# A block for overfull experts moves in front of expert 29 of a 32-expert layer

## The chip, the cores and the metric

One core of one Trainium2 chip runs one program. The metric is the device time of one execution in microseconds (us). An execution is profiled once more; its time and its span (first to last instruction) are given below.

## The reference

One layer of a flow-matching backbone on 256 latent tokens and 256 context tokens, width 1024. The first sub-layer (three token mixers and their merge) is untouched by this change. The second is a mixture of experts on the 256 latent tokens: a router takes the top 4 of 32 experts for each token, and every expert is a clamped SwiGLU with weights of its own.

```python
gate, up = jnp.split(h @ wgu + bgu, 2, axis=-1)      # 1024 -> 2 x 1024
gate = jnp.minimum(gate, SWIGLU_LIMIT)
up = jnp.clip(up, -SWIGLU_LIMIT, SWIGLU_LIMIT)
glu = gate * jax.nn.sigmoid(SWIGLU_ALPHA * gate)
y = ((up + 1) * glu) @ wd + bd                       # 1024 -> 1024
acc = acc + cw[:, None] * y                          # cw is 0 for a token outside the expert
```

All weights are f32, 12 MB for an expert, so the layer reads about 400 MB of expert weights.

## The kernel before, in words

Tokens are packed: an expert works on up to 64 slots (SLOTS). A token's place in an expert is counted by matmuls beforehand (posq); the number of tokens of each expert stands in cnt[0:32], and the largest of them in cnt[32]. A loop written out over the 32 experts, e = 0 to 31 (so "expert 29" is the 30th), does for each:

- gate_up (L1397): 16 steps (8 blocks of 128 rows, 2 column halves) into one PSUM bank, for the first half of gate and up, and 16 for the second; the bias is a matmul that opens the bank (biases, L1391).
- act (L1402 to L1406): the SwiGLU on VectorE (DVE) and ScalarE (ACT); turn (L1411, L1412): two transposes on TensorE (PE) and a copy on ACT.
- down (L1419): 2 times 16 steps into a bank, then spread (L1422 to L1424: DVE, ACT, DVE), which scales the result and splits it into two parts, and scatter (L1431), 8 matmuls that add it to four accumulator banks acc. The scatter of expert e-1 stands behind the first gate_up of expert e (L1496, L1497).
- gather (L1372): packs the tokens of the next pair of experts, inside the down step.
- select (L1364) marks the slots of tokens 65 to 128 of the expert; a run-time branch over PE, DVE and ACT (L1508 and L1524) computes them only where the expert has over 64 tokens.

Weights: a queue written out in order is loaded by SyncE (SP), one DMA of 2 MB for each of an expert's six pieces: gu e,0 to gu e,3 and dn e,0 and dn e,1 (smaller pieces for the last expert). There are nine slots of 2 MB. done(key) frees a slot at the place in the program where its last reader stands, and pump() issues the next DMA of the queue there and then (L166), so SP's instructions stand in that order. A load waits for the readers of its slot and, since DMAs take eight completion counters in turn, for the landing of the DMA eight before it.

Behind the loop stands the block for experts with over 128 tokens (L1565): a branch on most (the register that holds cnt[32], loaded at L1492) on PE, DVE, ACT and SP. Inside it, for each of the 32 experts, is a second branch, 12 DMAs of 1 MB into the free slots (room), and the computation of tokens 129 to 192 and 193 to 256. With these inputs no expert has over 128 tokens, so the block is jumped over. An engine that jumps executes, behind the branch, event-semaphore instructions that wait for a counter to have its value from before the block and then raise it by what the block would have added. Then come the final layer norm on acc (stats3 L1584, norm2 L1591 and L1592, a half on ACT and GpSimd, L1600 and L1602) and four DMAs of the output.

Of the kernel before, what the change touches and what calls it, by code (L numbers as in the profile page):

```python
# [17 lines left out]
ALU = mybir.AluOpType  # L18
AX = mybir.AxisListType
ET = mybir.EngineType  # L20
# [4 lines left out]
NE = 32  # L25
SLOTS = 64
# [91 lines left out]
def kernel(ctx, tc, x, cx, cols, rows, csts, wsm, wgt, bada, brt, sgub, bdn, bgu,  # L118
                           lnr, wad0, wada, win, wbr, wout, wgu, wdn, out):
    nc = tc.nc  # L120
    mm = nc.tensor.matmul
    V, S, G, T = nc.vector, nc.scalar, nc.gpsimd, nc.tensor
# [24 lines left out]
    loaded = {}  # L147
# [31 lines left out]
    def halves(*key):  # L179

        w = weight(key)
        return [w[:, 0:2048], w[:, 2048:4096]]
# [47 lines left out]
    with ExitStack() as p1:  # L230
# [159 lines left out]
        g2q = cst.tile([P, 512], F32, name="g2q")  # L390
# [937 lines left out]
    def sps2():  # L1328
        sbank.append(sbank.pop(0))
        return sbank[-1]  # L1330
# [26 lines left out]
    ysum = Buf(A2, 512)  # L1357
# [5 lines left out]
    def select(sl, n, c, e):  # L1363
        V.tensor_tensor(out=sl, in0=iota[:, None, None, SLOTS * c:SLOTS * c + SLOTS].to_broadcast([P, 2, n, SLOTS]),  # L1364
                        in1=posq[:, :, e:e + n].unsqueeze(3).to_broadcast([P, 2, n, SLOTS]), op=ALU.is_equal)
# [21 lines left out]
    def bias_of(e):  # L1387
        V.tensor_copy(out=bse[e % 2][:].rearrange("p (q n) -> p q n", q=2), in_=bsel[:, e, :].unsqueeze(2).to_broadcast([P, 2, SLOTS]))
# [11 lines left out]
    def act(b, hf, pg):  # L1400
        gc = b["gc"][hf]
        V.tensor_scalar_min(gc[:], pg[:, 0:256], LIMIT)  # L1402
        S.activation(out=sg[:], in_=gc[:], func=AF.Sigmoid, scale=SW_ALPHA)  # L1403
        V.tensor_scalar(out=up[:], in0=pg[:, 256:512], scalar1=LIMIT, scalar2=-LIMIT, op0=ALU.min, op1=ALU.max)  # L1404
        V.tensor_tensor(out=gc[:], in0=gc[:], in1=sg[:], op=ALU.mult)
        V.scalar_tensor_tensor(out=gc[:], in0=up[:], scalar=1.0, in1=gc[:], op0=ALU.add, op1=ALU.mult)  # L1406
# [14 lines left out]
    def spread(b, py):  # L1421
        V.scalar_tensor_tensor(out=ysum[:], in0=py[:], scalar=b["cwv"][:, 0:1], in1=g2q[:], op0=ALU.mult, op1=ALU.mult)  # L1422
        S.copy(out=yhx[:], in_=ysum[:])  # L1423
        V.tensor_tensor(out=ylx[:], in0=ysum[:], in1=yhx[:].bitcast(F32), op=ALU.subtract)  # L1424

    def scatter(b, last=False):
        for t in range(2):
            for hf in range(2):
                sl = slice(64 * hf, 64 * hf + 64)
                for y_ in (yhx, ylx):  # L1430
                    mm(acc[t][hf][:], b["sT"][sl, P * t:P * t + P], y_[sl, :], start=False, stop=last and y_ is ylx,  # L1431
                       skip_group_check=True)
# [12 lines left out]
    def scatter_whole(b, y, last):  # L1445
        for t in range(2):
            for hf in range(2):
                sl = slice(64 * hf, 64 * hf + 64)
                mm(acc[t][hf][:], b["sT"][sl, P * t:P * t + P].bitcast(F32), y[sl, :], start=False, stop=last, skip_group_check=True)

    def rest(e, g, wu, wd, end=False):
        turn(over, 0)
        biases(e, 1, g)
        gate_up(over["hT"][:, :, 0, :], g, range(8), wu)
        act(over, 1, g)
        py = sps2()
        down(over, py, range(4), wd)
        turn(over, 1)
        down(over, py, range(4, 8), wd)
        if end:  # L1460
            V.scalar_tensor_tensor(out=ysum[:], in0=py[:], scalar=over["cwv"][:, 0:1], in1=g2q[:], op0=ALU.mult, op1=ALU.mult)
            scatter_whole(over, ysum, False)
        else:
            spread(over, py)
            scatter(over)


    engs = [ET.PE, ET.DVE, ET.Activation]
# [15 lines left out]
    for e in range(NE):  # L1484
        p = pair[e // 2 % 2]
        q_ = pair[(e // 2 + 1) % 2]
        hT = p["hT"][:, :, e % 2, :]
        w = halves("gu", e, 0) + halves("gu", e, 1)
        select(over["sl"][:], 1, 1, e)
        _, (tv,) = nc.values_load_multi_w_load_instructions(cnt[0:1, e:e + 1], engines=engs, min_val=0, max_val=256)  # L1490
        if e == NE - 1:
            _, (most,) = nc.values_load_multi_w_load_instructions(cnt[0:1, NE:NE + 1], engines=[*engs, ET.SP], min_val=0, max_val=256)  # L1492
        g0, g1 = gbank if e % 2 == 0 else gbank[::-1]
        gate_up(hT, g0, range(8), w)
        act(cur, 0, g0)
        if e:  # L1496
            scatter(cur)  # L1497
        if e == NE // 2:
            for hf in range(2):
                sl = slice(64 * hf, 64 * hf + NE)  # L1500
                V.tensor_tensor(out=bdnt[sl], in0=bdnt[sl], in1=g2q[sl], op=ALU.mult)
        if e == NE - 4:
            for hf in range(2):
                sl = slice(64 * hf, 64 * hf + NE)
                for t in range(2):
                    mm(acc[t][hf][:], cwT[sl, P * t:P * t + P], bdnt[sl], start=False, stop=False, skip_group_check=True)
        over["hT"] = q_["hT"][:, 4:8].rearrange("p k (i j) n -> p (k i) j n", j=1)
        with tc.If(tv > SLOTS):  # L1508
            rest_gate(e, w)
        for i in range(2):  # L1510
            done(("gu", e, i))
        wu = halves("gu", e, 2)
        wu += halves("gu", e, 3) if e < NE - 1 else [weight(("gu1", e, i)) for i in range(2)]
        biases(e, 1, g1)
        gate_up(hT, g1, range(4), wu)
        spots(cur, p["sl"][:, :, e % 2, :], e)
        turn(cur, 0)
        gate_up(hT, g1, range(4, 8), wu)
        act(cur, 1, g1)
        if e < NE - 1:  # L1520
            wd = halves("dn", e, 0) + halves("dn", e, 1)
        else:
            wd = [weight(("dn1", e, i)) for i in range(4)]
        with tc.If(tv > SLOTS):  # L1524
            rest(e, g1, wu, wd)
        for key in [("gu", e, 2), ("gu", e, 3)] if e < NE - 1 else [("gu", e, 2), ("gu1", e, 0), ("gu1", e, 1)]:
            done(key)
        if e + 1 < NE:
            bias_of(e + 1)
        if e % 2 == 0 and e + 2 < NE:  # L1530
            select(q_["sl"][:], 2, 0, e + 2)
        down(cur, g0, range(4), wd)
        for key in [("dn", e, 0)] if e < NE - 1 else [("dn1", e, 0), ("dn1", e, 1)]:
            done(key)
        turn(cur, 1)
        if e + 2 - e % 2 < NE:
            gather(q_, e % 2, 2)
        if e + 1 < NE:
            biases(e + 1, 0, g1)
        down(cur, g0, range(4, 8), wd)  # L1540
        for key in [("dn", e, 1)] if e < NE - 1 else [("dn1", e, 2), ("dn1", e, 3)]:
            done(key)
        if e < NE - 1:
            spread(cur, g0)
        else:
            ylast, lnb = Buf(A, 512), Buf(A, 2, D)
            for i in range(2):
                S.dma_start(out=lnb[:, i, :], in_=lnr[2 + i:3 + i, :].to_broadcast([P, D]))
            V.scalar_tensor_tensor(out=ylast[:], in0=g0[:], scalar=cur["cwv"][:, 0:1], in1=g2q[:], op0=ALU.mult, op1=ALU.mult)
            scatter_whole(cur, ylast, True)  # L1550
        if e == 0:
            for hf in range(2):
                S.dma_start(out=bdnt[64 * hf:64 * hf + NE], in_=bdn[:, 512 * hf:512 * hf + 512])
        if e == NE - 6:
            ps = sps2()
            for hf in range(2):
                for t in range(2):
                    mm(ps[64 * hf:64 * hf + NE, P * t:P * t + P], cw[:, t], ident[:], start=True, stop=True)
            for hf in range(2):
                V.tensor_copy(out=cwT[64 * hf:64 * hf + NE], in_=ps[64 * hf:64 * hf + NE, 0:256])  # L1560

    engs = [*engs, ET.SP]
    room = [sp.slot() for sp in spaces for _ in range(sp.wlimit)]
    room = [r for r in room if r is not None]
    with tc.If(most > 2 * SLOTS):  # L1565
        for e in range(NE):
            _, (tv,) = nc.values_load_multi_w_load_instructions(cnt[0:1, e:e + 1], engines=engs, min_val=0, max_val=256)
            with tc.If(tv > 2 * SLOTS):
                for i, src in enumerate([wgu[e, i] for i in range(4)] + [wdn[e, i] for i in range(2)]):
                    for j in range(2):  # L1570
                        nc.sync.dma_start(out=room[2 * i + j], in_=src[:, 2048 * j:2048 * j + 2048])
                bias_of(e)
                for c in (2, 3):
                    select(over["sl"][:], 1, c, e)
                    rest_gate(e, room[0:4])
                    rest(e, gbank[0], room[4:8], room[8:12], True)


    S.activation(out=rs2[:, 0:1], in_=lneps[:, 0:1], func=AF.Sqrt)
    o = [[room[2 * t + hf][:, 0:512] for hf in range(2)] for t in range(2)]  # L1580
# [108 lines left out]
```

## Time and profile before

| | us |
|---|---|
| Runs of the kernel before | 1282.16, 1279.19, 1281.83; median 1281.83 |
| The profiled execution, its own time | 1278.06 |
| Its span, first to last instruction | 1276.3 |
| PE busy | 1184.0 (93%) |
| DVE busy | 462.5 (36%) |
| ACT busy | 285.2 (22%) |
| DMA | 471.74 MB, mean 370 GB/s |

The expert loop fills most of the span. PE busy is the time in which at least one matmul runs; PEq is PE's instruction sequencer, SPq that of SyncE. An instruction shown with "<-" was idle before, and the name behind the arrow is what released it.

### The profile page before, as it was taken

Reading aid. Unit: us, or ns where it says so; the run is one execution under the profiler, and the core shown is the slowest. Engines: PE = TensorE matmul, PEld = TensorE weight load, DVE = VectorE, ACT = ScalarE, POOL = GpSimd, SP = SyncE. Lnnn points to the kernel's source line nnn. Section 1 sums busy time; section 2 is a strip of 40 time slices with the busy share of each in tenths; the row PEclk is TensorE's granted clock in tenths of the full one; section 3 lists DMA queues with packets and bytes.
Section 4 is the critical chain, followed back from the end, with each engine's and each line's share of the span. In section 5 each row is a group of like instructions: output and inputs, shape, how many; then the busy total and the mean of one; then the engine's idle time right before and its main releaser. Section 6 shows DMA issues by size and latency. Waiting matters only on the chain. (4 is left out here: it accounts for less than half of the span.)

```text
span 1276.3 us, 16505 instructions
## 1 busy us (share of the span) xinstructions
PE 1184.0 (93%) x6619; PEld 609.9 (48%) x6624; DVE 462.5 (36%) x988; ACT 285.2 (22%) x548; POOL 28.4 (2%) x42
## 2 busy tenths in 40 slices
PE   7997999998999999999999999999898998889885
PEld 5897889996333334334433333333333333333321
DVE  6478758796322222222212222222222122222223
ACT  5352655734111111111111111111111111111101
POOL 1000000102000000000000000000000000000000
PEclk9998999998999999999999999999999999999998
DMA  9745657778899999999969999999999999999994
GB/s 390 270 151 215 218 194 284 293 306 322 354 425 426 426 426 427 426 379 428 375 238 386 428 426 427 426 425 427 427 427 426 425 426 427 427 426 425 428 422 179
DMA packets 39758, 471.74 MB, mean 370 GB/s; under 512 B 4561, under 2 KB 4689, under 8 KB 7761
## 3 DMA queue, kind: packets, MB, share of 16 engines
q1 hardware_dynamic: 37440, 464.01, 87.9%
q10 hardware_dynamic: 1552, 4.14, 1.0%
q8 instruction: 89, 1.46, 0.5%
q0 software_dynamic: 640, 1.84, 0.4%
q14 instruction: 37, 0.30, 0.1%
HBM read 468.92 MB, written 1.05 MB: 368 GB/s over the span
## 5 line engine op out<-in xcount | busy, mean ns | idle before, releaser
L1397 PE MATMUL bank<-arena,arena 128*64 128x512 f32 x1808 | 408.9, 596 | 18.1 <-DMA arena<-in_wgu_dram 17.5
L1419 PE MATMUL bank<-arena,arena 128*64 128x512 f32 x1088 | 248.3, 597 | 25.1 <-DMA arena<-in_wdn_dram 17.8
L1397 PEld LDWEIGHTS bank<-arena,arena 128*64 128x64 f32 x1808 | 124.0, 137 | 259.8 <-issue 235.2
L1419 PEld LDWEIGHTS bank<-arena,arena 128*64 128x64 f32 x1088 | 78.6, 136 | 171.9 <-issue 148.9
L251 PE MATMUL bank<-rounded 128*128 128x256 f32 (+1 forms) x1152 | 149.5, 289 | 0.1
L251 PEld LDWEIGHTS bank<-rounded 128*128 128x128 f32 x1152 | 143.9, 195 | 1.8 <-issue 0.6
L1402 DVE TENSOR_SCALAR arena<-bank 128x256 f32<-128x256 f32 x68 | 28.9, 425 | 279.1 <-PE bank L1397 279.1
L1422 DVE SCALAR_TENSOR_TENSOR arena<-bank,arena,g2q 128x512 f32<-128x512 f32 x33 | 24.8, 751 | 266.7 <-PE bank L1419 147.0
L1403 ACT ACTIVATE arena<-arena 128x256 f32<-128x256 f32 x68 | 28.5, 419 | 364.5 <-DVE arena L1402 360.6
L1412 ACT COPY arena<-bank 128x256 f32<-128x256 f32 x68 | 25.4, 373 | 290.5 <-PE bank L1411 290.5
L1397 PE MATMUL bank<-arena 128*64 128x512 f32 x368 | 83.7, 597 | 3.7 <-DMA arena<-in_wgu_dram 3.4
L348 DVE TENSOR_TENSOR rounded<-arena,rounded 128x2048 fp32r<-128x2048 f32 x29 | 66.3, 2285 | 15.1 <-ACT rounded L343 15.1
L1372 PE MATMUL bank<-arena 128*128 128x128 f32 (+1 forms) x576 | 69.9, 275 | 0.0
L1372 PEld LDWEIGHTS bank<-arena 128*128 128x128 f32 x576 | 66.9, 192 | 0.8 <-DVE arena L1404 0.7
L1375 ACT ACTIVATE arena<-bank,shc 128x128 f32<-128x128 f32 (+1 forms) x144 | 53.4, 452 | 51.4 <-PE bank L1372 51.4
L343 ACT CAST rounded<-arena 128x2048 fp32r<-128x2048 f32 x29 | 55.1, 1899 | 11.4 <-PE bank L251 5.6
L1384 DVE TENSOR_SCALAR rounded<-bank 128x256 fp32r<-128x256 f32 x34 | 14.5, 425 | 116.1 <-PE bank L1383 116.1
L1397 PEld LDWEIGHTS bank<-arena 128*64 128x64 f32 x368 | 24.9, 137 | 53.3 <-issue 44.3
L1423 ACT CAST rounded<-arena 128x512 fp32r<-128x512 f32 x33 | 20.4, 619 | 109.4 <-DVE arena L1422 109.4
L1431 PE MATMUL bank<-rounded 64*128 64x512 f32 x264 | 40.7, 418 | 3.6 <-ACT rounded L1423 3.1
L1431 PEld LDWEIGHTS bank<-rounded 64*128 64x128 f32 x264 | 22.8, 184 | 33.9 <-issue 25.1
L1391 PE MATMUL bank<-rounded 128*128 128x512 f32 x68 | 32.4, 476 | 5.8 <-PEq L1508 3.7
(326 smaller groups left out, 890.3 us busy)
## 6 DMA issues: line engine op xcount, KB each, us to landing
arena<-in_wgu_dram SPq DMA_DIRECT2D x127, 2048.0 KB, 29.6
arena<-in_wdn_dram SPq DMA_DIRECT2D x62, 2048.0 KB, 28.0
arena<-in_win_dram SPq DMA_DIRECT2D x23, 1024.0 KB, 5.1
arena<-in_wada_dram SPq DMA_DIRECT2D x16, 1024.0 KB, 5.0
arena<-in_wad_dram SPq DMA_DIRECT2D x8, 1024.0 KB, 10.8
arena<-in_wbr_dram SPq DMA_DIRECT2D x4, 1024.0 KB, 5.6
arena<-in_wout_dram SPq DMA_DIRECT2D x4, 1024.0 KB, 5.6
arena<-in_wdn_dram SPq DMA_DIRECT2D x3, 1024.0 KB, 29.4
```

The source lines that it names most:

```text
L251: mm(o, l, r, start=start and n == 0, stop=stop and n == len(todo) - 1)
L343: S.copy(out=wh[:, 0:2048], in_=w)
L348: V.tensor_tensor(out=wl[:, 0:2048], in0=w, in1=wh[:, 0:2048].bitcast(F32), op=ALU.subtract)
L1372: mm(pg[:, w * k:w * k + w], h2[:, t, 512 * a + P * k:512 * a + P * k + P], b["sl"][:, t].rearrange("p i n -> p (i n)"), start=t == 0, sto ...
L1375: S.activation(out=b["hT"][:, 4 * a + k].rearrange("p i n -> p (i n)"), in_=pg[:, w * k:w * k + w], func=AF.Identity, scale=shc[:, 1, 4 * ...
L1391: mm(pg[:], bse[e % 2][:], bst[:, hf, :], start=True, stop=False, skip_group_check=True)
L1397: mm(pg[64 * q:64 * q + 64, :], hT[:, k, :], wk[:, k % 2, 512 * q:512 * q + 512], start=False, stop=k == KB - 1, skip_group_check=True)
L1402: V.tensor_scalar_min(gc[:], pg[:, 0:256], LIMIT)
L1403: S.activation(out=sg[:], in_=gc[:], func=AF.Sigmoid, scale=SW_ALPHA)
L1412: S.copy(out=b["gT"][:, 4 * hf:4 * hf + 4, :].rearrange("p (q j) n -> p j q n", q=2), in_=pt[:, 0:256].rearrange("p (j q n) -> p j q n", j ...
L1419: mm(py[64 * q:64 * q + 64, :], b["gT"][:, k, :], wk[:, k % 2, 512 * q:512 * q + 512], start=k == 0, stop=k == KB - 1)
L1431: mm(acc[t][hf][:], b["sT"][sl, P * t:P * t + P], y_[sl, :], start=False, stop=last and y_ is ylx, skip_group_check=True)
```

## The change: what it does

The block becomes a function, many(e, g), called once, in front of expert 29 (e == NE - 3). It no longer has slots of its own: it borrows the two slots that hold dn 29,0 and dn 29,1 (four halves of 1 MB), loads through them the weights of an overfull expert in three portions for each of its two token groups, and at its end loads dn 29,0 and dn 29,1 again. The load of most into registers moves there too, and the scatter of expert 28 moves to just in front of the call, so ahead of expert 29's first gate_up.

```diff
+    def many(e, g):
+        w = halves("dn", e, 0) + halves("dn", e, 1)
+        engs_ = [*engs, ET.SP]
+        _, (most,) = nc.values_load_multi_w_load_instructions(cnt[0:1, NE:NE + 1], engines=engs_, min_val=0, max_val=256)
+        def fetch(srcs):
+            for i, src in enumerate(srcs):
+                for j in range(2):
+                    nc.sync.dma_start(out=w[2 * i + j], in_=src[:, 2048 * j:2048 * j + 2048])
+        with tc.If(most > 2 * SLOTS):
+            for x_ in range(NE):
+                _, (tv,) = nc.values_load_multi_w_load_instructions(cnt[0:1, x_:x_ + 1], engines=engs_, min_val=0, max_val=256)
+                with tc.If(tv > 2 * SLOTS):
+                    bias_of(x_)
+                    for c in (2, 3):
+                        fetch([wgu[x_, i] for i in range(2)])
+                        select(over["sl"][:], 1, c, x_)
+                        rest_gate(x_, w)
+                        fetch([wgu[x_, i] for i in range(2, 4)])
+                        rest_up(x_, g, w)
+                        fetch([wdn[x_, i] for i in range(2)])
+                        py = rest_down(w)
...
+                        scatter_whole(over, ysum, False)
+            bias_of(e)
+            for i in range(2):
+                nc.sync.dma_start(out=loaded["dn", e, i][0], in_=wdn[e, i])
...
+        g0, g1 = gbank if e % 2 == 0 else gbank[::-1]
+        if e == NE - 3:
+            scatter(cur)
+            many(e, g1)
         select(over["sl"][:], 1, 1, e)
         _, (tv,) = nc.values_load_multi_w_load_instructions(cnt[0:1, e:e + 1], engines=engs, min_val=0, max_val=256)
-        if e == NE - 1:
-            _, (most,) = nc.values_load_multi_w_load_instructions(cnt[0:1, NE:NE + 1], engines=[*engs, ET.SP], min_val=0, max_val=256)
-        g0, g1 = gbank if e % 2 == 0 else gbank[::-1]
         gate_up(hT, g0, range(8), w)
         act(cur, 0, g0)
-        if e:
+        if e and e != NE - 3:
             scatter(cur)
...
-    with tc.If(most > 2 * SLOTS):
-        for e in range(NE):
-            _, (tv,) = nc.values_load_multi_w_load_instructions(cnt[0:1, e:e + 1], engines=engs, min_val=0, max_val=256)
-            with tc.If(tv > 2 * SLOTS):
-                for i, src in enumerate([wgu[e, i] for i in range(4)] + [wdn[e, i] for i in range(2)]):
-                    for j in range(2):
-                        nc.sync.dma_start(out=room[2 * i + j], in_=src[:, 2048 * j:2048 * j + 2048])
-                bias_of(e)
-                for c in (2, 3):
-                    select(over["sl"][:], 1, c, e)
-                    rest_gate(e, room[0:4])
-                    rest(e, gbank[0], room[4:8], room[8:12], True)
```

rest is cut into rest_up and rest_down, with the same instructions for the ordinary branch.

## Rows read from the trace of the kernel before

**Rows 1.** Stretches: us, busy (count) by PE, PEld, DVE, ACT, POOL, clock, DMA share, GB/s.
```profile
480.00:520.00 40.00, 39.53 (x206) 17.07 (x206) 10.36 (x27) 6.76 (x19) 0.00 (x0) 1.00 1.01 426
...
1160.00:1240.00 80.00, 69.52 (x333) 25.92 (x333) 17.05 (x43) 9.17 (x22) 0.00 (x0) 1.00 1.01 427
```
**Rows 2.** PE in order of time, experts 28 to 30: start, us, what.
```profile
1169.80 3.65 PE L1419 MATMUL bank<-arena,arena 128*64 128x512 f32 x16
1173.28 3.60 PE L1397 MATMUL bank<-arena,arena 128*64 128x512 f32 x16
...
1187.82 3.65 PE L1397 MATMUL bank<-arena 128*64 128x512 f32 x16 [0.20 <-DMA arena<-in_wgu_dram]
1194.17 3.65 PE L1419 MATMUL bank<-arena,arena 128*64 128x512 f32 x16 [2.70 <-DMA arena<-in_wdn_dram]
```
**Rows 3.** The block's line L1565, all engines: duration ns min/median/max, first and last start.
```profile
L1565 SPq EVENT_SEMAPHORE  x9: 17/17/17, 1244.4 to 1261.3; - x9
...
L1565 PEldq COMPARE_BRANCH  x1: 3609/3609/3609, 1260.5 to 1260.5; - x1
```
**Rows 4.** Everything in order of time, end of the loop and start of the norm.
```profile
1251.47 3.65 PE L1419 MATMUL bank<-arena,arena 128*64 128x512 f32 x16 [0.31 <-PEq L1524]
...
1255.96 3.65 PE L1419 MATMUL bank<-arena,arena 128*64 128x512 f32 x16 [0.46 <-ACT arena L1412]
...
1260.46 1.99 PE L1449 MATMUL bank<-arena,rounded 64*128 64x512 f32 x8 [0.85 <-DVE arena L1549]
...
1261.59 1.28 ACT L1579 ACT_TABLE_LOAD   x1 [5.68 <-ACTq L1565]
...
1264.24 1.29 DVE L1584 BATCH_NORM_STATS2 st<-bank 128x6 f32<-128x512 f32 x2 [3.83 <-PEq L1565]
```
**Rows 5.** The block's line on SP, from 1245 to 1261.1 and from 1261 to 1262.
```profile
L1565 SPq EVENT_SEMAPHORE  x5: 17/17/17, 1255.2 to 1261.1; - x5
...
L1565 SPq EVENT_SEMAPHORE  x4: 17/17/17, 1261.1 to 1261.3; - x4
```
**Rows 6.** DMAs issued at 1228.20 and 1223.31: KB, us from issue to landing.
```profile
arena<-in_wdn_dram SPq DMA_DIRECT2D x1, 1024.0 KB, 27.0
...
arena<-in_wdn_dram SPq DMA_DIRECT2D x1, 1024.0 KB, 29.4
```
**Rows 7.** SP in order of time from 1133: start of the first issue, us to the last's end.
```profile
1133.67 21.92 SPq L166 DMA_DIRECT2D arena<-in_wgu_dram  x4
1156.03 7.95 SPq L166 DMA_DIRECT2D arena<-in_wdn_dram  x2
1164.07 19.21 SPq L166 DMA_DIRECT2D arena<-in_wgu_dram  x4
```
**Rows 8.** DMAs issued at 1133.67 and 1173.49 (gu 29,0 and gu 30,2).
```profile
arena<-in_wgu_dram SPq DMA_DIRECT2D x1, 2048.0 KB, 39.4
...
arena<-in_wgu_dram SPq DMA_DIRECT2D x1, 2048.0 KB, 40.0
```
**Rows 9.** The page's DMA issues: the output's.
```profile
out_dram<-arena SPq DMA_DIRECT2D x4, 256.0 KB, 2.0
```
**Rows 10.** PE in order of time over one early expert, weights already there.
```profile
357.26 3.65 PE L1419 MATMUL bank<-arena,arena 128*64 128x512 f32 x16 [0.31 <-PEq L1524]
...
366.72 7.04 PE L1397 MATMUL bank<-arena,arena 128*64 128x512 f32 x32
...
383.57 0.65 PE L1419 MATMUL bank<-arena,arena 128*64 128x512 f32 x2 [0.31 <-PEq L1524]
```
**Rows 11.** Stretches with PE idle or just restarted; columns as in Rows 1.
```profile
120.80:127.60 6.80, 4.97 (x19) 4.63 (x20) 3.64 (x9) 2.17 (x2) 0.00 (x0) 0.50 0.73 298
...
1262.50:1267.70 5.20, 0.00 (x0) 0.00 (x0) 3.35 (x9) 1.86 (x5) 0.00 (x0) 1.00 0.02 5
1267.70:1276.00 8.30, 0.00 (x0) 0.00 (x0) 5.08 (x7) 0.08 (x1) 2.85 (x2) 0.50 0.34 127
```
**Rows 12.** PE in order of time around 122.
```profile
122.63 2.06 PE L586 MATMUL bank<-arena 128*128 128x258 f32 x4 [4.28 <-DVE arena L578]
```

More of the change, by code (lines that the diff above doesn't have):

```diff
@@ L1449, in scatter_whole, with rest_up @@
                 mm(acc[t][hf][:], b["sT"][sl, P * t:P * t + P].bitcast(F32), y[sl, :], start=False, stop=last, skip_group_check=True)
-    def rest(e, g, wu, wd, end=False):
+    def rest_up(e, g, wu):
         turn(over, 0)
@@ L1455, in rest, with rest_down @@
         act(over, 1, g)
+    def rest_down(wd):
         py = sps2()
@@ L1459, in rest @@
         down(over, py, range(4, 8), wd)
[L1460 to L1465, printed above, removed]
+        return py
+    def rest(e, g, wu, wd):
+        rest_up(e, g, wu)
+        spread(over, rest_down(wd))
+        scatter(over)
+    def many(e, g):
[19 more added lines that the diff above has]
+                        py = rest_down(w)
+                        V.scalar_tensor_tensor(out=ysum[:], in0=py[:], scalar=over["cwv"][:, 0:1], in1=g2q[:], op0=ALU.mult, op1=ALU.mult)
+                        scatter_whole(over, ysum, False)
+            bias_of(e)
+            for i in range(2):
+                nc.sync.dma_start(out=loaded["dn", e, i][0], in_=wdn[e, i])
     engs = [ET.PE, ET.DVE, ET.Activation]
@@ L1560 @@
                 V.tensor_copy(out=cwT[64 * hf:64 * hf + NE], in_=ps[64 * hf:64 * hf + NE, 0:256])
-    engs = [*engs, ET.SP]
     room = [sp.slot() for sp in spaces for _ in range(sp.wlimit)]
     room = [r for r in room if r is not None]
-    with tc.If(most > 2 * SLOTS):
-        for e in range(NE):
-            _, (tv,) = nc.values_load_multi_w_load_instructions(cnt[0:1, e:e + 1], engines=engs, min_val=0, max_val=256)
-            with tc.If(tv > 2 * SLOTS):
-                for i, src in enumerate([wgu[e, i] for i in range(4)] + [wdn[e, i] for i in range(2)]):
-                    for j in range(2):
-                        nc.sync.dma_start(out=room[2 * i + j], in_=src[:, 2048 * j:2048 * j + 2048])
-                bias_of(e)
-                for c in (2, 3):
-                    select(over["sl"][:], 1, c, e)
-                    rest_gate(e, room[0:4])
-                    rest(e, gbank[0], room[4:8], room[8:12], True)
     S.activation(out=rs2[:, 0:1], in_=lneps[:, 0:1], func=AF.Sqrt)
```

## The prediction, written before the result was known

> **What bounds the kernel now.** I read the page (PE 93% busy), then stretches, PE in order of time, and the block's own line on each engine. The DMA engines are full in both stretches shown, but what that means differs: early in the expert loop PE is the limit (busy 39.5 of 40 us), late in it DMA is (DMA share 1.01, PE busy 69.5 of 80 us, so about 13% slack) [rows 1]. The change falls into the second kind. Around expert 29 PE takes each piece about when it lands: down of expert 28 ends at 1173.45, the first gate_up of 29 starts at 1173.28, and down of 29 waits 2.70 us for its weights [rows 2]. So a short hole in PE there costs nothing if loads keep flowing, and a hole in the loads costs all of itself. The end is no longer DMA-bound: the last down runs from its copies, then DVE scales, PE scatters until 1262.45, and the norm starts at 1264.24, released by PE's sequencer at the block's line [rows 4].
>
> **What the move takes away.** At the end PE's jump over the block takes 3.609 us from 1260.48 [rows 3]. It begins under the scatter, so the norm starts 1.8 us after PE's last matmul. Without it each acc bank can be normed as its two parts are added: the first pair of the eight scatter matmuls is done about a third into their 1.99 us, some 1261.2, and DVE needs 0.65 us a bank (1.29 for two), more than the 0.5 us (a quarter of 1.99) in which PE makes one. DVE then starts at 1261.2 instead of 1264.24: 3.0 us. If PE signals only after the whole scatter, 1.8. I take 3.0, since each bank has its own reader in the norm. ACT's table load, which waited 5.68 us for ACT's jump [rows 4], moves ahead with it and stays off the path. Nothing else at the end holds the norm.
>
> **What it adds in front of expert 29, on PE, DVE and ACT.** The scatter of 28 now waits for spread, which starts when down 28 ends at 1173.45; three short instructions of DVE and ACT, and the scatter itself, bring PE to about 1177, an estimate. Then the jump, 3.6 us, and gate_up 29 from about 1181.5 instead of 1173.3. Its pieces land meanwhile, so PE makes the first half without a wait, and the second, which cannot end before its last piece of 1187.8, ends near 1198 instead of 1191.5 [rows 2]. Next is down 29. If that started at its old 1194.17, the hole would cost at most 4 us there and be taken back from the 13% slack; cover gone, 3.6 us for the jump. I cost it at nothing because of what follows, which is later still.
> The Trainium skill (Runtime: NRT & Kernel Launch, section Instruction fetch mechanics) says that a taken branch to code outside the fetched window stalls until that code is loaded; the 3.609 us agree, and by that rule the price goes with the jump and is not saved by moving it, only covered.
>
> **What it adds on SP: the decisive part.** SP jumps too, because the block loads weights. Behind the jump SP had nine event semaphores [rows 3]: one of its own and one for each of the eight DMA completion counters. They are executed one by one, in a fixed order, and each waits until its counter has everything that was issued before the block. The first counter was raised at 1255.2 [rows 5], which is the landing of the DMA issued at 1228.20 (27.0 us later) [rows 6]; the last four came together at 1261.1 to 1261.3 [rows 5], though one of them belongs to the DMA issued at 1223.31, which landed 29.4 us later, at 1252.7 [rows 6]. It waited for its turn behind slower ones. At the end that cost nothing: SP had no load left to issue.
> In front of expert 29 it has eight in flight. Which ones: done of dn 28,1 frees a slot just before the call, and the load that takes it is gu 30,2, the third of the four issues from 1164.07, at 1173.49 [rows 7]. Counting back eight issues (three of gu 30, two of dn 29, three of gu 29 before them) gives 1133.67, gu 29,0, whose counter it shares, landed 39.4 us later at 1173.1 [rows 7, 8]. gu 30,2 itself lands 40.0 us after its issue, at 1213.5 [rows 8]. So SP passes its jump near 1180, waits until 1213.5, and all loads that before were issued after 1173.49 and up to 1213.5 go out behind that. DMA runs dry for the time from an issue to its first bytes, an estimate of 2.5 us (the output's small DMAs take 2.0 from issue to landing [rows 9]).
>
> **Why PE stops.** The block rewrites the slots of dn 29 at its end, so down 29 must wait for the counters of those two reloads, which SP raises after the jump. Eight counters in turn: the 24 block DMAs of an expert are a multiple of eight, so the two reloads take the counters that follow gu 30,2's. In the order of the trace counter one is that of 1228.20, and going back in steps of eight it is that of gu 29,3; gu 30,2 has the sixth, the reloads the seventh and eighth. These are raised last, after the sixth: at 1213.6. Down 29 then starts at 1213.7 instead of 1194.17, 19.5 us later, though the first of its weights landed then.
>
> **How much PE takes back.** From 1213.7 the other pieces are there or come in time (gu 30,0 to 2 in SBUF; from 1213.6 a 2 MB piece each 4.9 us, gu 30,3 near 1221, needed at 1239; slots of gu 29 are all free), so PE goes at its own pace. That is read early in the loop: down with gather 9.46 us (357.26 to 366.72), gate_up to down 16.85 (366.72 to 383.57) [rows 10]. Down without gather, as for experts 30 and 31, is 8.14 (1251.47 to 1259.61) [rows 4]. From the start of down 29 to the end of down 31: 9.46 + 16.85 + 8.14 + 16.85 + 8.14 = 59.4 us; before it took 1259.61 - 1194.17 = 65.4. PE takes back 6.0: 19.5 - 6.0 = 13.5 late.
>
> **The clock.** PE idles from about 1198 to 1213.7. After the last matmul the granted clock stayed at 1.00 for 5.2 us and was then 0.50, 1.2 instead of 2.4 GHz [rows 11]. After an idle stretch of 4.28 us PE restarted at 122.63, the clock at 0.50 until 127.60 [rows 11, 12]: 5.0 us at half pace lose 2.5. Ends: 0 (the clock does not fall) and 3.4 (the whole 6.8 us stretch); I take 2.5, the row nearest in kind.
> The Trainium skill (TensorE: Matmul & The Clock Gate, section HAM oscillation — how this bites in real kernels) tells of a kernel that has 1.67 us throttled after each DMA wait, half of which is lost. By that the term would be 0.8 and the sum 11.3; the 5.0 us of the row are longer.
>
> **Sum.** 19.5 - 6.0 + 2.5 - 3.0 = +13.0 us. Against the profiled execution's 1278.06 that is 1291.1. The runs lie 1.1 to 4.1 above that execution; on their median, 1281.83, it is 1294.8. I forecast 1294.5. Ends of its terms: clock 0 to 3.4, end of kernel 1.8 to 3.0, take-back 6.0 give or take 1.5: +9.0 to +16.6; with the median's own spread 1288.5 to 1299.
>
> **Rivals.**
> A, *SP drains, PE does not stop* (0.11): down 29 keeps its old counters, or those raised early (the first stands at gu 29,3's landing, 1187.8). Then only the hole in the loads counts, +2.5, since the stretch is DMA-bound, and the end gives 3.0 back: -0.5, 1281.3. This is the side of "not slower"; it decides if the counters that down 29 waits for are raised before 1194. Against it: a reader of a rewritten slot cannot go by the old load alone.
> B, *SP does not hold the loads up* (0.06): if its raises can be made without the landings, or the waits overlap, the eight loads in flight cover its jump of some 5 us, and only the end counts: 1281.8 - 3.0 = 1278.8; with a take-back of the moved scatter's place perhaps 1277.5. Against it are the raise times that equal landings [rows 5, 6].
> C, *the reloads have earlier counters* (0.07): each step nearer the front of the order is one landing, 4.9 us, earlier: +8.1 or +3.2 and less clock loss, 1284 to 1290.
> D, *the change does not take the jump off the end* (0.02): the 3.0 stay, 1297.5.
> The forecast has 0.74.
>
> **How the numbers follow.** A measurement of this kernel can tell about 0.3% (3.9 us) from no change. Slower by more: the forecast, D and nearly all of C, with a little of A: 0.81. Same: A, and most of B: 0.15. Faster: the rest of B, 0.04. The forecast's own range with most of C reaches 8 in 10: 1284 to 1299.
>
> **What would show it.** Right: SP issues no load between about 1173.5 and 1213.6, then several at once; the DMA share falls to nothing for some 2 us there; PE idle for 15 us in front of the first L1419 of expert 29, released by SP's sequencer at the If; clock 0.50 for a few us behind it; no DMA waits of PE in experts 30 and 31; the norm starts under 1 us after the first scatter matmul. Wrong: down 29 starting within 5 us of 1194 (then A or B), loads issued by SP between 1180 and 1210 (B), or PE waiting for loads again in experts 30 and 31, which would make it over 1299.

## The result, and the profile after

The kernel after takes 1293.49 us (median of 6 runs, 1289.13 to 1295.79), the kernel before 1280.69 (6 runs, 1278.16 to 1282.16): ratio 1.0104, 95% interval 1.0086 to 1.0121, so 12.8 us slower. The profiled execution took 1293.44 us, its span is 1291.7.

The trace after, PE in order of time from expert 28 on; these answer to [rows 2] and [rows 4] (columns: start, us, what; in brackets the idle time before and what ended it; "..." marks lines left out):

```profile
1172.21 3.65 PE L1419 MATMUL bank<-arena,arena 128*64 128x512 f32 x16
1177.44 0.49 PE L1431 MATMUL bank<-rounded 64*128 64x512 f32 x1 [1.57 <-ACT rounded L1423]
...
1185.69 9.69 PE L1397 MATMUL bank<-arena,arena 128*64 128x512 f32 x32 [6.34 <-PEq L1526]
...
1200.11 3.65 PE L1397 MATMUL bank<-arena 128*64 128x512 f32 x16
1216.02 6.45 PE L1419 MATMUL bank<-arena,arena 128*64 128x512 f32 x16 [12.25 <-SPq L1480]
...
1224.79 3.65 PE L1419 MATMUL bank<-arena,arena 128*64 128x512 f32 x16
1228.27 7.04 PE L1397 MATMUL bank<-arena,arena 128*64 128x512 f32 x32
...
1274.46 3.65 PE L1419 MATMUL bank<-arena,arena 128*64 128x512 f32 x16 [0.46 <-ACT arena L1412]
```

Expert 29's first gate_up starts at 1185.69 behind the spread, the scatter and the jump; its second ends at 1203.76; then PE stands 12.25 us until SP's sequencer releases it at L1480, which is the block's branch in this kernel. What follows runs without one wait for a load, at the pace of [rows 10].

The block's line, all engines (duration ns min/median/max, first and last start); answers to [rows 3]:

```profile
L1480 SPq EVENT_SEMAPHORE  x9: 17/17/17, 1182.5 to 1215.9; - x9
...
L1480 SPq EVENT_SEMAPHORE  x5: 17/17/17, 1191.4 to 1210.9; - x5
...
L1480 SPq EVENT_SEMAPHORE  x3: 17/17/17, 1215.8 to 1215.9; - x3
...
L1480 SPq COMPARE_BRANCH  x1: 50/50/50, 1177.2 to 1177.2; - x1
...
L1480 PEldq COMPARE_BRANCH  x1: 6024/6024/6024, 1178.6 to 1178.6; - x1
...
  PE bank L1419: 12.3, 1
```

SP branches at 1177.2 and raises its nine semaphores between 1182.5 and 1215.9 (the x5 and x3 lines are the same view from 1190 to 1215 and from 1215 to 1217). The first raise, at 1182.5, is that of its own semaphore. The next six come one by one, at 1191.4, 1196.3, 1201.2, 1206.1, 1210.9 and 1215.8, each within 0.2 us of the landing of one load in the order of issue, from gu 29,3 to gu 30,2. The last two, whose loads were issued ahead of gu 29,3, follow at once. That is the order the prediction counted out, with the reloads of dn 29 on the last two. SP's waits there (us in total, times, longest):

```profile
SPq L1480 <- SPq L1480: 38.6, 7, 8.9
```

38.6 us in seven waits is the whole time from the branch to the last raise: 5.3 us to the first raise, the rest for landings. No load goes out in it. The DMA issued last in front of the branch, gu 30,2, lands 39.9 us behind its issue at 1175.91, at 1215.8:

```profile
arena<-in_wgu_dram SPq DMA_DIRECT2D x1, 2048.0 KB, 39.9
```

SP in order of time shows the gap inside a merged row: four gu loads, of which the first three go out at 1166.48 to 1175.91 and the fourth at 1216.06 (the row's 49.92 us), and behind it two dn loads in 0.83 us:

```profile
1166.48 49.92 SPq L166 DMA_DIRECT2D arena<-in_wgu_dram  x4
1216.52 0.83 SPq L166 DMA_DIRECT2D arena<-in_wdn_dram  x2
```

Stretches (us, busy and count by PE, PEld, DVE, ACT, POOL, granted clock, DMA share, GB/s); they answer to [rows 1] and [rows 11]:

```profile
1180.70:1190.90 10.20, 5.21 (x14) 1.56 (x16) 0.29 (x1) 0.00 (x0) 0.00 (x0) 0.50 1.00 414
...
1200.00:1208.00 8.00, 3.76 (x18) 1.06 (x16) 2.59 (x7) 0.79 (x2) 0.00 (x0) 1.00 0.92 389
1208.00:1216.00 8.00, 0.00 (x0) 0.01 (x1) 0.00 (x0) 0.00 (x0) 0.00 (x0) 0.50 0.45 190
...
1215.00:1217.00 2.00, 0.98 (x4) 0.43 (x6) 0.00 (x0) 0.00 (x0) 0.00 (x0) 0.50 0.00 0
...
1216.00:1222.00 6.00, 5.98 (x16) 1.93 (x16) 0.00 (x0) 0.00 (x0) 0.00 (x0) 0.53 0.83 311
...
1208.00:1221.70 13.70, 5.68 (x14) 1.94 (x16) 0.00 (x0) 0.00 (x0) 0.00 (x0) 0.50 0.59 233
1221.70:1260.00 38.30, 37.60 (x183) 13.89 (x179) 7.97 (x19) 4.70 (x11) 0.00 (x0) 1.00 1.01 426
```

The clock is at 0.50 (1.2 GHz) twice in this part: once from 1180.7, 1.4 us into the hole of the jump, for 10.2 us, and again from 1208, 4.2 us after PE's last matmul, until 1221.7, 5.7 us after its restart. The DMA share sinks to 0.45 in the last 8 us of the drain (the time in which the loads in flight land and no new one is issued). From 1221.7 on the stretch is PE's: busy 37.6 of 38.3 us.

The end: the last scatter starts at 1278.97, the norm 1.16 us later, released by PE's matmul and not by a jump (before: 3.78 us, [rows 4]).

```profile
1280.13 1.30 DVE L1602 BATCH_NORM_STATS2 st<-bank 128x6 f32<-128x512 f32 x2 [1.21 <-PE bank L1449]
```

### The profile page after: what moved, and what is told of

It is laid out like the page before. It is cut to its first block, busy times and chain, and to the rows that moved or that the text cites. A ratio compares the mean times of both kernels' runs of the same rounds, so it can differ in the third digit from the quotient of the medians.

```text
span 1291.7 us, 16509 instructions
## 1 busy us (share of the span) xinstructions
PE 1188.1 (92%) x6624; PEld 609.9 (47%) x6624; DVE 462.1 (36%) x988; ACT 284.9 (22%) x548; POOL 28.3 (2%) x42
```

## The experiments

Ratios are to the kernel before on the same chip, with the 95% interval. There before had a median of 1281.11 us for experiments 1 to 4, 1280.71 for experiments 5, 6, 8 and the first run of 7, and 1280.74 for the other two runs of 7.

**1. The end alone.** The kernel before without the block and without the load of most.

```diff
-        if e == NE - 1:
-            _, (most,) = nc.values_load_multi_w_load_instructions(...)
...
-    with tc.If(most > 2 * SLOTS):
...
```

> The kernel before without the block behind the loop and without the load of most (an expert with over 128 tokens would lose tokens). Theory: the jump at the end kept the norm from starting under the scatter, so the time is 3 us below before, about 1277.6. Rival, the jump is hidden under PE's last matmuls and the table load: within 1 us of before.

Measured: 1276.84 us, ratio 0.9967 (0.9951 to 0.9984), 4.3 us below before with an interval from 2 to 6. The norm starts 1.16 us behind the start of the scatter (1265.12 to 1266.28) where before it took 3.78, and from the end of the last down to the end of the span is 13.6 us (1264.26 to 1277.9) where before it was 16.7:

```profile
1260.61 3.65 PE L1419 MATMUL bank<-arena,arena 128*64 128x512 f32 x16 [0.46 <-ACT arena L1412]
...
1265.12 1.99 PE L1449 MATMUL bank<-arena,rounded 64*128 64x512 f32 x8 [0.86 <-DVE arena L1547]
...
1266.28 1.29 DVE L1569 BATCH_NORM_STATS2 st<-bank 128x6 f32<-128x512 f32 x2 [1.22 <-PE bank L1449]
```

So the gain that the change was credited with at the end is real, and of the size forecast: 3.1 us in the trace.

**2. No loads in the block, SP not in it.**

```diff
-        engs_ = [*engs, ET.SP]
+        engs_ = [*engs]
...
-                        fetch([wgu[x_, i] for i in range(2)])
...
-            for i in range(2):
-                nc.sync.dma_start(out=loaded["dn", e, i][0], in_=wdn[e, i])
```

> The kernel after with all DMAs taken out of the block and SP out of its branches (an overfull expert would be computed with wrong weights). PE, DVE and ACT still jump in front of expert 29. Theory, all of the loss hangs on SP: about 14 us below after. PE's own hole there (wait for spread, jump of 6 us, lower clock) made PE 7.4 us late in the trace of after, of which 6.1 are taken back, so 1.3 stays and the end gives 3.1 back: 1.8 us below before, 1279. Rival, the hole on PE counts in full: 4 us above before.

Measured: 1278.71 us, ratio 0.9985 (0.9970 to 1.0001). PE still jumps in front of expert 29, and down 29 starts without a wait for SP:

```profile
1186.45 8.52 PE L1397 MATMUL bank<-arena,arena 128*64 128x512 f32 x32 [6.35 <-PEq L1521]
...
1203.67 3.65 PE L1419 MATMUL bank<-arena,arena 128*64 128x512 f32 x16 [0.31 <-PEq L1552]
```

All of the loss hangs on the block's loads and SP's part in it: the time lies between nothing and 4 us below before. Experiment 1, which has the same end and no hole on PE, is 1.9 us faster, and the two intervals overlap: what PE's own hole costs here is about 2 us by the medians, not clear of the noise.

**3. Other counters for the reloads, a miss.**

```diff
             bias_of(e)
+            for i in range(2):
+                nc.sync.dma_start(out=w[i % 4], in_=wdn[e, 0][:, 0:2048])
             for i in range(2):
                 nc.sync.dma_start(out=loaded["dn", e, i][0], in_=wdn[e, i])
```

> The kernel after with two more 1 MB loads inside the block, in front of the two reloads, so that the reloads have the first and the second completion counter in SP's order instead of the seventh and eighth. SP still waits for all eight landings. Theory, the release of down 29 is what costs: it starts near 1204 in the time of the trace of after instead of 1216, and only the hole in the loads of some 2.5 us stays; between 1 us below and 2 us above before, 1280 to 1283. Rival, the held loads alone cost: no change from after, 1293.

Measured: 1293.75 us, ratio 1.0102 (1.0080 to 1.0124): no change. The trace:

```profile
1215.17 6.43 PE L1419 MATMUL bank<-arena,arena 128*64 128x512 f32 x16 [12.34 <-SPq L1480]
```

Down 29 still waits for SP's last raises. My edit was at fault: the two added loads write into the borrowed slots as well, and by the count they took the counters that the reloads had. My reading is that a reader behind the block waits for every load in it that writes its slot, not only for the last one; no run here tests that by itself. So the run fits the rival by its number but decides nothing; experiments 5 and 6 ask the same question in another way.

**4. The block's loads on GpSimd.** Complete: nothing is left out.

```diff
-        engs_ = [*engs, ET.SP]
+        engs_ = [*engs, ET.Pool]
...
-                    nc.sync.dma_start(out=w[2 * i + j], ...)
+                    nc.gpsimd.dma_start(out=w[2 * i + j], ...)
...
-                nc.sync.dma_start(out=loaded["dn", e, i][0], in_=wdn[e, i])
+                nc.gpsimd.dma_start(out=loaded["dn", e, i][0], in_=wdn[e, i])
```

> The kernel after with the block's loads issued by GpSimd instead of SP, and GpSimd in its branches instead of SP; nothing is left out. These loads have counters of their own, on which nothing is in flight there. Theory: nobody waits for a landing, SP goes on issuing, and the time is that of the run without loads, 1.8 us below before, 1279. Rival, whoever jumps over the loads waits for those in flight whatever its queue: as after, 1293.

Measured: 1277.90 us, ratio 0.9977 (0.9960 to 0.9994). GpSimd had been through its jump for over 860 us when the others came to theirs, and its raises took 0.8 us. The block's line, then the stretch that in the kernel after holds the stop:

```profile
L1480 POOLq EVENT_SEMAPHORE  x5: 17/43/43, 317.6 to 317.9; - x5
...
L1480 POOLq INC_SWDGE_SEM  x1: 397/397/397, 318.0 to 318.0; - x1
...
L1480 PEldq COMPARE_BRANCH  x1: 5991/5991/5991, 1182.1 to 1182.1; - x1
```

```profile
1190.00:1230.00 40.00, 39.26 (x187) 14.64 (x185) 9.18 (x24) 4.49 (x11) 0.00 (x0) 0.97 1.01 426
```

The wait belongs to the counters, not to the jump: on counters with nothing in flight there is none. (GpSimd also came to its branch long before the others, so this run alone doesn't tell its counters from its early hour; experiment 6 keeps SP and the place.)

**5. The same block, slots that are read one step later.** Complete as well.

```diff
-        w = halves("dn", e, 0) + halves("dn", e, 1)
+        w = halves("gu", e + 1, 0) + halves("gu", e + 1, 1)
...
-                nc.sync.dma_start(out=loaded["dn", e, i][0], in_=wdn[e, i])
+                nc.sync.dma_start(out=loaded["gu", e + 1, i][0], in_=wgu[e + 1, i])
```

> The kernel after, but the block borrows (and loads again) the two slots of gu 30,0 and gu 30,1 instead of those of dn 29; nothing is left out, and SP still waits for all eight landings. Down 29 then reads slots that the block doesn't touch. Theory, the loss is PE's wait for the raise in front of what reads the borrowed slots: it moves from down 29 to the first gate_up of 30, 1216 on the clock of the trace of after, where PE arrives at 1213.4 by itself; PE is 12 us earlier than in after, and the clock does not fall for it: within 2 us of before, 1280 to 1283. Rival, the held loads alone cost: as after, 1293.

Measured: 1281.01 us, ratio 1.0011 (0.9992 to 1.0030). SP is held as long as in the kernel after, and down 29 runs through; PE meets the raise where it nearly would have been anyway:

```profile
L1480 SPq EVENT_SEMAPHORE  x9: 17/17/17, 1178.1 to 1211.5; - x9
```

```profile
1199.88 3.65 PE L1419 MATMUL bank<-arena,arena 128*64 128x512 f32 x16 [0.31 <-PEq L1557]
...
1211.55 7.09 PE L1397 MATMUL bank<-arena,arena 128*64 128x512 f32 x32 [2.05 <-SPq L1480]
...
1240.27 3.65 PE L1397 MATMUL bank<-arena,arena 128*64 128x512 f32 x16 [0.21 <-DMA arena<-in_wgu_dram]
```

This takes the two halves of the mechanism apart. SP's drain with all its held loads is there in full, and the whole costs what the end gives back, some 3 us. Even of these the trace puts little down to missing loads: PE waits 2.05 us for the raise, and behind it only 0.21 us for a load. The other 12 us of the kernel after are PE's wait in front of the borrowed slots, with the clock that falls in it. Which slots the block borrows sets its price here.

**6. Only two counters to raise.** The reloads are the only loads left in the block.

```diff
-                        fetch([wgu[x_, i] for i in range(2)])
...
-                        fetch([wgu[x_, i] for i in range(2, 4)])
...
-                        fetch([wdn[x_, i] for i in range(2)])
```

> The kernel after with the twelve loads of each token group taken out and only the two reloads of dn 29 left in the block, SP still in its branches (an overfull expert would be computed with wrong weights). SP then has two completion counters to raise instead of eight, those of gu 29,1 and gu 29,2, which land near 1180 and 1185. Theory, SP waits only for the counters that the block's loads use: SP is free by 1186, the loads go on, PE is not held: 2 us below before, 1279. Rival, a branch with SP in it drains all loads in flight whatever it holds: as after, 1293.

Measured: 1277.80 us, ratio 0.9976 (0.9959 to 0.9994). SP now has three semaphores, its own and two, and is free at 1186.2:

```profile
L1480 SPq EVENT_SEMAPHORE  x3: 17/17/17, 1178.8 to 1186.2; - x3
```

So SP waits for the counters that the block's loads would have used, and for no others.

**7. The clock.** PE is kept busy while it waits, with zero-adding matmuls.

```diff
+        if e == NE - 3:
+            idle2(acc[0][0][:], 56)
         if e + 1 < NE:
             bias_of(e + 1)
```

> The kernel after with 56 matmuls that add zero to an accumulator bank (bf16, 512 columns) in front of down 29, in PE's idle stretch of 12 us. Theory, the clock falls in that stretch and the first half of down 29 takes 6.45 instead of 3.65 us for it: with PE busy there the clock stays at 2.4 GHz and the time is 2.8 us below after, 1290.5 (9.5 us above before). Rival, the 6.45 us have another cause: as after, or slower by what the 56 matmuls run over.

Measured: 1292.11 us, ratio 1.0083 (1.0053 to 1.0112). In the trace the first half of down 29 takes 3.65 us, but the 56 matmuls ended at 1218.8, 0.5 us behind SP's last raise at 1218.3. With 50, and the kernel after beside it on the same chip:

> The kernel after, unchanged, as the partner of the next run on the same chip: 12 to 13 us above before, and the first half of down 29 takes over 6 us.

> The kernel after with 50 instead of 56 zero-adding matmuls in front of down 29, about 11 us, so that they end before SP's raise (the 56 ended 0.5 us behind it). Theory, the clock term of the sum is real: 2.8 us below the kernel after of the same chip, the first half of down 29 3.65 us. Rival, the clock costs nothing in the total because PE takes it back behind: the same as the kernel after within 1 us.

Measured: after 1295.15, ratio 1.0102 (1.0080 to 1.0125); with 50 matmuls 1290.46, ratio 1.0080 (1.0057 to 1.0103). The partner's trace, then the trace with 50:

```profile
1218.71 5.33 PE L1419 MATMUL bank<-arena,arena 128*64 128x512 f32 x16 [13.33 <-SPq L1480]
```

```profile
1204.53 11.05 PE L1335 MATMUL bank<-zb,identb 128*128 128x512 bf16 x50 [0.16 <-PEq L1557]
1216.39 3.65 PE L1419 MATMUL bank<-arena,arena 128*64 128x512 f32 x16 [0.81 <-SPq L1480]
```

```profile
1216.00:1222.00 6.00, 5.61 (x35) 3.29 (x35) 0.00 (x0) 0.38 (x1) 0.00 (x0) 1.00 0.78 270
```

The clock stays at 1.00, and the step is 2.8 us shorter than in the first trace of after (6.45) and 1.7 shorter than in the partner's (5.33). PE does not take this back: from the start of down 29 to the end of the span is 72.9 us with 50 matmuls (span 1289.3), 75.7 in the first trace of after and 74.6 in the partner's (span 1293.3). The ratios differ by 0.0022, 2.8 us, and the medians by 4.7, but the intervals overlap, so the traces show the term and the times only fit it. The expectation for the partner run missed in one point: its first half of down 29 took 5.33 us, not over 6. The loss varies from run to run, here between 1.7 and 2.8 us.

**8. A version that beats both.** The block's loads on GpSimd, the call in front of expert 23, the scatter in its old place; complete.

```diff
-        if e == NE - 3:
-            scatter(cur)
+        if e == NE - 9:
             many(e, g1)
...
-        if e and e != NE - 3:
+        if e:
             scatter(cur)
```

> The run with the block's loads on GpSimd, with the call moved from expert 29 to expert 23 and the scatter back to its old place behind the first gate_up; nothing is left out. Theory: PE's hole is then the jump alone, in a stretch bound by the loads, with 8 experts behind it to take it back, so only the gain of the end is left: as the run without the block, 3 to 4 us below before, 1277. Rival, the hole is not taken back wherever it stands: 1 us below before or more.

Measured: 1277.04 us, ratio 0.9974 (0.9955 to 0.9993), 3.7 us below before and 16 below after. PE's hole there is the jump, with a slower gate_up behind it (9.56 us, for 7.04 in [rows 10]):

```profile
1001.79 9.56 PE L1397 MATMUL bank<-arena,arena 128*64 128x512 f32 x32 [4.44 <-PEq L1525]
```

It is faster than before by 0.3%, with an interval that ends at 0.9993. Whether it is faster than experiment 4 (0.9977) the runs do not tell.

## Why the prediction was right

The forecast was 1294.5 and +13.0 us over the profiled execution; measured 1293.49, and 12.8 us between the medians. (The forecast stood on the first three runs of before, median 1281.83; all six have 1280.69, which accounts for the 1.0 us by which it came out high.) Its terms, read from the two profiled executions:

| Term | Forecast | Trace |
|---|---|---|
| Down 29 starts later | 19.5 | 19.4 |
| PE takes back | -6.0 | -6.15 |
| Clock | 2.5 | 2.8 |
| End | -3.0 | -3.1 |
| Sum | 13.0 | 13.0 |

How they are read: down 28's second half starts at 1172.21 instead of 1169.80 [rows 2], so the execution after was already 2.4 us behind where the programs begin to differ on PE; the runs of one kernel differ by that much and more. Down 29 starts at 1216.02 instead of 1194.17, 21.85 later, less these 2.4. From there to the end of the last down is 62.09 us (1216.02 to 1278.11) instead of 65.44; without the 2.8 us that its first step is longer (6.45 against 3.65) it is 59.3, against 59.4 forecast. From the last down to the end of the span is 13.6 us instead of 16.7. With the 2.4 the spans differ by 15.4, the medians by 12.8.

- *SP holds its loads until gu 30,2 has landed*: right, and shown by the trace; that it comes from the counters which the block's loads would raise, by experiments 4 and 6. Rival B (SP doesn't hold the loads up) is out for this kernel, and is what experiment 4 builds: 1277.9 against its 1278.8.
- *PE stops because the block rewrites the slots of dn 29*: right. Experiment 5 is rival A built on purpose, loads held but PE hardly so: 1281.0 against its 1281.3. That the two agree so closely is luck, since A's 2.5 us were for missing loads and the trace has 2.05 us of waiting for the raise. PE's wait was 12.25 us and not the 15 foreseen, because PE came to it later.
- *The order of the raises decides, reloads last*: the raises came in the order counted, and the release with the last of them. That the reloads' counters alone decide was too simple: in experiment 3 they should have stood first and second, and down 29 waited for the last raises all the same. If readers wait for the block's other loads into their slot as well, which would explain it and isn't shown, rival C has no ground, and the count of the reloads' place was not needed.
- *PE's hole in front of expert 29 costs nothing*: right in sum, its size was wrong. The jump took 6.02 us there against 3.609 at the end [rows 3], and the clock fell in this hole too, so gate_up 29 took 9.69 us for 7.04 [rows 10]. The second gate_up ended at 1203.76, or 1201.4 without the 2.4 us, where the forecast had 1198. The 12 us of waiting behind it cover that; in experiment 2, without the wait, it is part of the 1.9 us that separate that run from experiment 1.
The Trainium skill (Runtime: NRT & Kernel Launch, section Instruction fetch mechanics) says that such a jump stalls until the target code is loaded. The traces agree, with 3.6 us where the DMA engines are nearly idle and 5.9 to 6.6 where they are full; how much of it is loading no run separates.
- *The DMA engines run dry for 2.5 us*: mis-sized. The share is nothing for the 2 us foreseen (0.00 from 1215 to 1217), but it had been sinking since 1206. By the stretches above, 1200 to 1222 lost some 6 us of full rate, an estimate from their shares. It did not count here, because PE was the later of the two from 1216 on.
- *The clock*: 2.8 in this trace, 1.7 in the partner run. The forecast took 2.5 from a single earlier row; that it lies between the two is in part luck.
By the figures that the Trainium skill (TensorE: Matmul & The Clock Gate, section HAM oscillation — how this bites in real kernels) gives for another kernel, 1.67 us throttled after each wait and half of it lost, the estimate was 0.8. The two traces measure more, and they decide.
- *The end*: right in sum. The norm started 1.16 us behind the start of the scatter, not under 1 as foreseen, which is 2.6 of the 3.1 us; the other 0.5 lie inside the norm, from its start to the end of the span (12.1 us before, 11.6 after).

## What to carry to other kernels

In this kernel a jumped-over block was not free for the engine that would have issued its DMAs: it waited until every completion counter that the block would raise had caught up with what was in flight, and the reader of what the block writes waited for that raise. So let an issuer with nothing in flight hold such a block, or borrow what is read last, and count the loads in flight at the place before moving it there. In a stretch bound by loads a hole of some us on PE came back for the most part (experiment 2). The held load queue, with a wait of 2 us, cost some 3 us (experiment 5), and the wait in front of a buffer the other 12.

## What the runs showed of the hardware

- The same kind of jump on PE took 3.6 us at the end of the kernel, where the DMA engines were nearly idle (12 GB/s from 1260.4 to 1264.2), and 5.9 to 6.6 us in front of expert 29 (6.02 after; 6.57, 6.09, 5.91, 5.99 in experiments 7, 5, 6 and 4) and 6.32 in front of expert 23, where they were full (416 GB/s during the jump in the kernel after). Both jumps have packets of the instruction queues in the trace, 4 and 5. That the fetch of the code queues behind the loads would explain the difference; no run separates that from the other code around the jump.
- This drain of the load queue was not a short gap: the DMA share went 0.92, 0.45, 0.83 over 22 us (1200 to 1222) for one stop of the issuer.
- With PE holes of 1.57 us in front of the scatter and 6.34 us behind it, the granted clock fell to 0.50 at 1180.7, in the second of them, and stayed there for 10.2 us.
- The clock can fall without the change too. In the trace of experiment 1 the first half of down 29 took 5.00 us behind its ordinary wait for weights, the clock at 0.50 from 1198.6 to 1201; before, behind nearly the same wait (2.70 us), it took 3.65 [rows 2].

```profile
1198.63 5.00 PE L1419 MATMUL bank<-arena,arena 128*64 128x512 f32 x16 [2.78 <-DMA arena<-in_wdn_dram]
```
